# Fifteen places in the weight ring, and the last expert unit added into x by 0/1 products

## The chip, the core and the metric

The kernel runs on one core of one Trainium2 chip. The metric is device time in microseconds, median of three runs. TensorE (PE) multiplies, with its weight loads listed as PEld; VectorE (DVE), ScalarE (ACT) and GpSimd (POOL) do elementwise work; SyncE (SP) issues most DMAs. Each engine works through its own instructions in order.

## The reference

Two transformer blocks over 512 tokens of width 1024. The change lies in the mixture of experts that ends the first block: 32 experts, two for each token, each a SwiGLU of 1024 to 512 to 1024.

```python
def hierarchical_moe(h, ...):              # h: 512 tokens x 1024
    g_idx = argmax(h @ w_rg + b_rg)        # one of 4 groups
    top_val, top_loc = top_k(e_logits of that group, 2)   # 2 of its 8 experts
    gates = softmax(top_val) * g_gate
    # per expert e: every token that chose it
    out = (silu(x @ w_gate[e]) * (x @ w_up[e])) @ w_down[e] * gate
    return sum over a token's two experts

def first_block(x, ...):
    x = x + gate_a * mix                   # adaLN, mLSTM heads and pooling, w_out
    x = x + gate_f * hierarchical_moe(rms_norm(x, norm2_g) * (1 + scale_f) + shift_f, ...)
    return rms_norm(x, final_g)

def second_block(x, ...):                  # per layer: mixer (gMLP, then attention) and SwiGLU
    x = x + gmlp_mixer(rms_norm_2(x, a_norm[0]), ...)
    ...
    return rms_norm_2(x, final_norm)
```

## The kernel before

The activations lie transposed in `xT`, [128, 8, 512]. The stages follow one another: a mixer (adaLN modulation, mLSTM heads, pooling, output projection), the router, the experts, an overflow loop, the combination with x, then gMLP, SwiGLU, attention and SwiGLU. The order on each engine is the order in which the Python code records the instructions; waits are put in between by the framework.

`route` writes the normalised tokens to DRAM (`h2d`, L1283), ranks the experts by load and makes tables: `gidx`, which token sits in each row of a unit, `sidx`, the row of `y2` to which its output goes, `ordi`, the place of each expert's weights. The 32 experts make 19 units of 128 rows (`UNITS`, NU = 19): thirteen units hold two experts of up to 64 tokens, six a single one. The first unit holds two fixed experts, whose weights can be loaded before the router is done. Tokens beyond a unit's rows go to `overflow` (L1578), a loop with a run-time count, which is zero for these inputs.

The weights of an expert are six tiles of 1 MB: four for gate and up (`gu`), two for the projection down (`down`), 192 tiles in all. `Ring` (L309) loads them on SP's queue into 12 places (the names t, r and w are buffers that other stages use as well); a tile is loaded when the tile 12 ahead of it in the ring's order has been used on PE. `fill` reads the expert's place from `ordi` on SP before the expert's first load.

In `experts` (L1485) unit n is gathered from `h2d` by an indirect DMA on POOL (`gather`, three buffers `xg`), turned on PE (`x_t`), multiplied by gate and up (`gu`), gated on ACT and DVE, turned again (`act_t`), multiplied by `down`; DVE multiplies each half by the gate row of the modulation into `yo`, and an indirect DMA on POOL writes the rows of `yo` to `y2` in DRAM, [1024, 1024]: a row for each token and each of its two choices (`scatter`). The products down of unit n stand behind gate and up of unit n + 1; those of the last unit come at the end.

After the loop, `combine` (L1633) reads `y2` back as eight tiles of 128 rows `ya` on the queues of SP and ACT. For each of four token tiles, `tile(t)` adds the two choices (POOL, the last one DVE), turns the sum on PE (L1659), adds it into `xT` (DVE), and splits the new x into a high and a low part (`ht`: ACT, then DVE), which gMLP's products need. `ahead` (L1700) calls `tile` between the first gMLP products, so tile t + 1 is handled while the products of tile t run. `Stream` (`ws`, L214) loads and splits the other stages' weights; the first two tiles of gMLP are loaded behind the ring's last.

Of the kernel before, what the change touches and what calls it, by code (L numbers as in the profile page):

```python
# [308 lines left out]
class Ring:  # L309


    PLACES = ("t0", "t1", "r1", "w2", "w3", "r0", "w0", "w1", "r2", "r3", "t2", "t3")

    def __init__(self, K):
        self.K, self.order, self.loaded, self.used, self.at, self.tiles = K, [], 0, 0, {}, {}
        self.order = [(p, c) for c in range(6) for p in UNITS[0]]
        for n in range(1, NU + 1):
            for cs, u in ((range(4), n), ((4, 5), n - 1)):
                if 0 < u < NU:
                    self.order += [(p, c) for c in cs for p in UNITS[u]]  # L320

    def fill(self, most=1000):
        K = self.K
        while self.loaded < min(most, len(self.order), self.used + len(self.PLACES)):
            i = self.loaded
            p, c = self.order[i]
            t = self.tiles[i] = K.sb(self.PLACES[i % len(self.PLACES)], [128, 2048])
# [6 lines left out]
            K.nc.sync.dma_start(t, src)  # L334
# [21 lines left out]
class Kern:  # L356
# [331 lines left out]

    def load_late(self):
# [7 lines left out]
    def mixer(self):  # L697
# [72 lines left out]
        for j in range(DT):  # L770
# [10 lines left out]
            if j == 3:  # L781
                self.load_late()
            if j == 7:
# [478 lines left out]
    def route(self):  # L1262
# [21 lines left out]
        self.xg = [self.slot(i, [128, D]) for i in range(3)]  # L1284
# [19 lines left out]
        sel = self.slot(9, [128, NT, 4, 8])  # L1304
# [35 lines left out]
        rkt = self.slot(9, [128, 2, NT, 32])  # L1340
# [4 lines left out]
        rkt = self.slot(9, [128, 2, NT, 32])  # L1345
# [17 lines left out]
        pay = self.slot(10, [128, 8, 2, NU], F32R)  # L1363
# [24 lines left out]
        self.ts(self.gidx, tab[:, 224:224 + NU], 1024.0, None, OP.add)  # L1388
        self.ts(self.sidx, tab[:, 224 + NU:224 + 2 * NU], 1024.0, None, OP.add)
# [3 lines left out]
        def later():  # L1393
# [18 lines left out]
            table(oh0.bitcast(F32), tab[:, 264:264 + NU], lambda k, t: unit[:, 1, k * NT + t])  # L1412
            self.gates = self.sb("gates", [128, NU + 96])
# [71 lines left out]
    def experts(self):  # L1485

        nc = self.nc
        self.y2 = self.dr.tile([2 * S, D], F32, name="y2")
# [16 lines left out]
        def x_t(n):  # L1505
            b = self.ps(1)
            x = self.xg[n % 3]
            for k in range(8):
                nc.tensor.transpose(b[:, k // 4, (k % 4) * 128:(k % 4) * 128 + 128], x[:, k * 128:(k + 1) * 128], self.const("ident"))
            t = XT[n] = self.slot(3 + n % 2, [128, D])  # L1510
            self.turned(t, b)

        def products(n, out, lhs, first, last):
# [3 lines left out]
            for i in range(4):  # L1517
                for t, p in zip(ts, c):
                    self.mm(out[p], lhs[:, i * 128 + p.start:i * 128 + p.stop], t[:, i * 512:i * 512 + 512], first and i == 0, last and i == 3)
# [6 lines left out]
        def act_t(n):  # L1526
# [4 lines left out]
            t = ACT[n] = self.slot(5 + n % 2, [128, 512])  # L1531
            self.act(t, b)

        def down(n):
# [576 lines left out]
```

## Time and profile before

| | us |
|---|---|
| median of three runs | 1924.69 (1922.97 to 1930.77) |
| the profiled execution | 1929.17 |
| its span in the profile | 1927.4 |
| PE busy | 1813.0 (94%) |
| DVE busy | 848.8 (44%) |
| ACT busy | 593.0 (31%) |
| POOL busy | 146.0 (8%) |

The profile follows one execution. The busy share is an average over stages with different limits: the mixer (to about 260 us) is a mesh of short waits among all engines, the experts (about 283 to 771 us) are a stream of weights, and from about 800 us PE runs nearly without gaps to the end. What a change in one stage is worth is read from that stage's own rows.

### The profile page before, as it was taken

The page shows a single profiled execution, that of the slowest core. Times are in us where ns is not written, and L with a number is a line of the kernel's source. Part 1 is how long each engine was busy: PE and PEld are TensorE (multiplying, and loading weights), DVE is VectorE, ACT ScalarE, POOL GpSimd, SP SyncE. Part 2 cuts the span into 40 slices and gives each one's busy share as a digit, 9 for nine tenths or more (in the row PEclk, how much of TensorE's full clock was granted, in tenths as well). Part 3 has the DMA queues.
Part 4 walks back from the last instruction along what each step waited for, and adds up shares of the span by engine and source line. Part 5 has one row for each costly group of instructions (what it writes and reads, how often), then busy time and mean ns, then how long its engine had stood idle before and what let it go on. Part 6 is the DMA issues. An engine that isn't in the chain of part 4 may idle for free.

```text
span 1927.4 us, 20923 instructions
## 1 busy us (share of the span) xinstructions
PE 1813.0 (94%) x8054; PEld 1267.0 (66%) x8054; DVE 848.8 (44%) x1566; ACT 593.0 (31%) x1054; POOL 146.0 (8%) x119
## 2 busy tenths in 40 slices
PE   5988779999999898699999999999999999999997
PEld 4856654434333333588888888888778788888885
DVE  7657851111121111767644334436555654424434
ACT  4556430000000000444423223226666433212221
POOL 3443320000000000200000000000000000000000
PEclk9988879999999999899999999999999999999998
DMA  7533579999999998422232322222111132222321
GB/s 242 214 110 131 214 288 417 420 420 420 421 420 419 418 417 346 176 88 88 87 110 88 109 88 88 99 77 88 66 66 66 66 110 88 94 104 88 109 77 55
DMA packets 61240, 360.92 MB, mean 187 GB/s; under 512 B 9730, under 2 KB 9762, under 8 KB 23763
## 3 DMA queue, kind: packets, MB, share of 16 engines
q1 hardware_dynamic: 54000, 347.78, 46.6%
q0 software_dynamic: 5696, 8.64, 1.3%
q10 hardware_dynamic: 1442, 3.15, 0.4%
q8 instruction: 64, 1.05, 0.2%
q14 instruction: 38, 0.30, 0.1%
HBM read 356.91 MB, written 14.16 MB: 193 GB/s over the span
## 4 chain that ended last, share of the span: by engine, by line
PE 58%; DVE 1%; DMA 1%; ACT 0%; issue 0%; ACTq 0%; POOL 0%; DVEq 0%; POOLq 0%
PE q L394 57%; PE q L1988 0%; DMA a<-y 0%; PE q L465 0%; DVE a L414 0%; DVE t L406 0%; DMA y<-a,sidx 0%; DVE w L414 0%; DVE xT L406 0%; PE q L1659 0%; DVE ht L414 0%; POOL a L1656 0%; DVE a L406 0%; ACT t L403 0%; ACTq L1645 0%
## 5 line engine op out<-in xcount | busy, mean ns | idle before, releaser
L394 PE MATMUL q<-t,w 128*128 128x512 f32 (+1 forms) x3192 | 767.3, 397 | 7.4 <-DVE t L406 2.6
L394 PEld LDWEIGHTS q<-t,w 128*128 128x128 f32 (+1 forms) x3192 | 596.1, 189 | 150.6 <-issue 16.2
L406 DVE TENSOR_TENSOR w<-r,w 128x1024 fp32r<-128x1024 f32 (+1 forms) x173 | 208.6, 1226 | 312.2 <-ACT w L403 312.1
L394 PE MATMUL q<-a,w 128*128 128x512 f32 x1440 | 339.1, 395 | 0.0
L394 PEld LDWEIGHTS q<-a,w 128*128 128x128 f32 x1440 | 269.6, 188 | 63.6 <-issue 1.0
L403 ACT ACTIVATE w<-r 128x1024 fp32r<-128x1024 f32 (+1 forms) x173 | 177.1, 1049 | 347.3 <-issue 177.9
L394 PE MATMUL q<-r,a 128*64 128x512 f32 (+4 forms) x576 | 207.4, 580 | 10.3 <-DMA r<-in_we 8.9
L394 PE MATMUL q<-w,a 128*64 128x512 f32 (+1 forms) x512 | 186.1, 596 | 11.3 <-DMA w<-in_we 10.6
L403 ACT ACTIVATE a<-q 128x512 f32<-128x512 f32 (+2 forms) x82 | 37.2, 482 | 453.1 <-PE q L1530 358.4
L394 PE MATMUL q<-t,a 128*64 128x512 f32 (+1 forms) x512 | 145.9, 600 | 8.9 <-DMA t<-in_we 7.9
L414 DVE SCALAR_TENSOR_TENSOR a<-a,gates,q 128x512 f32<-128x512 f32 x19 | 14.2, 747 | 282.8 <-PE q L394 282.8
L394 PEld LDWEIGHTS q<-r,a 128*64 128x64 f32 (+1 forms) x576 | 69.6, 150 | 97.9 <-issue 77.0
L394 PEld LDWEIGHTS q<-w,a 128*64 128x64 f32 (+1 forms) x512 | 61.4, 147 | 93.3 <-issue 71.5
L394 PE MATMUL q<-w,t 128*128 128x256 f32 (+1 forms) x672 | 122.0, 336 | 0.0
L394 PEld LDWEIGHTS q<-w,t 128*128 128x128 f32 x672 | 102.8, 191 | 17.9 <-issue 4.1
L394 PEld LDWEIGHTS q<-t,a 128*64 128x64 f32 (+1 forms) x512 | 50.1, 147 | 92.1 <-issue 72.3
L406 DVE TENSOR_TENSOR a<-q,sqt 128x512 f32<-128x512 f32 x38 | 26.3, 692 | 116.1 <-PE q L394 116.1
L403 ACT ACTIVATE a<-ht 128x512 fp32r<-128x512 f32 (+1 forms) x60 | 37.8, 633 | 99.3 <-DVE ht L406 74.6
L406 DVE TENSOR_TENSOR xT<-q,xT 128x512 f32<-128x512 f32 x64 | 43.8, 687 | 52.9 <-PE q L394 43.5
L414 DVE SCALAR_TENSOR_TENSOR w<-r,cols,w 128x256 fp32r<-128x256 f32 x96 | 44.4, 480 | 39.3 <-ACT w L403 39.1
L403 ACT ACTIVATE ht<-ht 128x512 f32<-128x512 f32 x48 | 30.1, 631 | 87.3 <-DVE ht L406 87.3
L1471 POOL DMA_INDIRECT y<-a,sidx x19 | 20.9, 1098 | 450.6 <-DVE a L406 340.7
(325 smaller groups left out, 1398.0 us busy)
## 6 DMA issues: line engine op xcount, KB each, us to landing
r<-in_w SPq DMA_DIRECT2D x100, 1024.0 KB, 4.9
t<-in_we SPq DMA_DIRECT2D x64, 1024.0 KB, 20.9
r<-in_we SPq DMA_DIRECT2D x64, 1024.0 KB, 20.9
w<-in_we SPq DMA_DIRECT2D x64, 1024.0 KB, 20.4
r<-in_w_ada SPq DMA_DIRECT2D x48, 512.0 KB, 5.0
r<-in_wa SPq DMA_DIRECT2D x8, 466.0 KB, 8.9
r<-in_w SPq DMA_DIRECT2D x5, 512.0 KB, 3.5
xT<-in_x SPq DMA_DIRECT2D x4, 512.0 KB, 4.4
```

What stands on the lines that cost most here:

```text
L394: self.nc.tensor.matmul(out, lhsT=l, rhs=r, start=start, stop=stop)
L403: return self.nc.scalar.activation(out, in_, f, **kw)
L406: return self.nc.vector.tensor_tensor(out=out, in0=a, in1=b, op=op)
L414: return self.nc.vector.scalar_tensor_tensor(out, a, s, b, op0=op0, op1=op1, **kw)
L1471: self.nc.gpsimd.indirect_dma_start(out=self.y2[:, :], out_offset=bass.IndirectOffsetOnAxis(ap=idx, axis=0), in_=y, in_offset=None, bounds ...
```

## The change

The ring gets three more places, each made of two slots of 512 KB, loaded by two DMAs. To free the slots, other buffers become fewer or move: two gather buffers for three, one buffer for the turned input, `yo` in slots 5 and 3, the router's scratch in other names. The ring's order changes at the end: the products down of unit 17 come ahead of gate and up of unit 18.

The outputs of the last unit are not scattered. A 0/1 matrix `hot` (row of the unit by token, from the new table `tok`) turns and places them by a product on PE that is added to the turned sum of the other units' rows in the same bank. `y2` is read back, on SP, before the last `down`, and the sums of the two choices move from POOL to DVE. As the last unit's rows of `y2` are now not written, `y2` is cleared in the mixer (`clear`). The overflow loop adds its outputs to `xT` in the same manner and stands behind the addition into x; `combine` keeps the split alone. Two loads of gMLP move from SP's queue to POOL's.

```diff
 class Ring:
-    PLACES = ("t0", "t1", "r1", "w2", "w3", "r0", "w0", "w1", "r2", "r3", "t2", "t3")
+    PLACES = ("t0", "t1", "r1", "w2", "w3", "r0", "w0", "w1", "r2", "r3", "t2", "t3", ("a8", "a9"), ("a10", "a11"), ("a6", "a7"))
...
-        for n in range(1, NU + 1):
-            for cs, u in ((range(4), n), ((4, 5), n - 1)):
-                if 0 < u < NU:
-                    self.order += [(p, c) for c in cs for p in UNITS[u]]
+        parts = [(range(4), 1)]
+        for n in range(2, NU - 1):
+            parts += [(range(4), n), ((4, 5), n - 1)]
+        for cs, u in parts + [((4, 5), NU - 2), (range(6), NU - 1)]:
+            self.order += [(p, c) for c in cs for p in UNITS[u]]
...
+            if isinstance(tags, str):
+                t = K.sb(tags, [128, 2048])
+                K.nc.sync.dma_start(t, src)
...
+            else:
+                self.tiles[i] = []
+                for h, tag in enumerate(tags):
+                    t = K.sb(tag, [128, 1024])
+                    K.nc.sync.dma_start(t, src[:, h * 1024:(h + 1) * 1024])
+                    self.tiles[i] += [t[:, :512], t[:, 512:]]
...
+    def clear(self):
+
+        self.y2 = self.dr.tile([2 * S, D], F32, name="y2")
+        for i in range(8):
+            self.nc.scalar.dma_start(self.y2[i * 128:(i + 1) * 128], self.zero)
...
             if j == 3:
                 self.load_late()
+                self.zero = self.slot(9, [128, D])
+                nc.gpsimd.memset(self.zero, 0.0)
...
                 self.act(vT[t][:, :, 129 * i:129 * i + 128], v[:, :, i])
+        self.clear()
...
+            self.ts(self.tok, tab[:, 224:224 + NU], 1024.0, None, OP.add)
...
-        self.nc.gpsimd.indirect_dma_start(out=self.xg[n % 3], out_offset=None, in_=self.h2d[:, :],
+        self.nc.gpsimd.indirect_dma_start(out=self.xg[n % 2], out_offset=None, in_=self.h2d[:, :],
...
-            t = XT[n] = self.slot(3 + n % 2, [128, D])
+            t = XT[n] = self.slot(2, [128, D])
...
-            self.scatter(yo, self.sidx[:, i:i + 1])
+                if g == 0 and between:
+                    between()
+            if n < NU - 1:
+                self.scatter(yo, self.sidx[:, i:i + 1])
+            return yo
...
-        self.ws.stop = self.wide + 2
-        self.ws.fill()
-        act_t(NU - 1)
-        down(NU - 1)
-        self.ws.hold = len(self.ws.order)
-        self.ws.run()
+
+        n = NU - 1
+        act_t(n - 1)
+        down(n - 1)
+        i = UCOL[UNITS[n][0]]
+        hot = self.sb("W", [128, S], bufs=2)
+        self.onehot(hot, self.tok[:, i:i + 1])
+        banks = self.ps(0)
+        gu(n, 0, banks)
+        gu(n, 1, banks)
+        gate(n, banks)
+        ya = [[self.slot((8, 9, 10, 11, 6, 7, 0, 1)[2 * t + k], [128, D]) for k in range(2)] for t in range(NT)]
+        for t in range(NT):
+            if t % 2 == 0:
+                self.ws.stop = self.wide + 1 + t // 2
+                self.ws.fill()
+            for k in range(2):
+                nc.sync.dma_start(ya[t][k], self.y2[k * S + t * 128:k * S + (t + 1) * 128])
+        act_t(n)
+
+        def split():
+            self.ws.hold = len(self.ws.order)
+            self.ws.run()
+
+        yo = down(n, split)
+        for t in range(NT):
+            c = slice(t * 128, (t + 1) * 128)
+            b = Pair(*[self.bank(i) for i in ((0, 1), (6, 7))[t % 2]])
+            for a in range(2):
+                y, y2 = (ya[t][k][:, a * 512:a * 512 + 512] for k in range(2))
+                self.tt(y, y, y2, OP.add)
+                for i in range(4):
+                    k = slice(a * 512 + i * 128, a * 512 + i * 128 + 128)
+                    self.mm(b[:, a, i * 128:i * 128 + 128], ya[t][0][:, k], self.const("ident"), True, False)
+                    self.mm(b[:, a, i * 128:i * 128 + 128], yo[:, k], hot[:, c], False, True)
+                x = self.xT[:, 4 * a:4 * a + 4, c]
+                self.tt(x, b[:, a].rearrange("p (b t) -> p b t", b=4), x, OP.add)
+
+    def onehot(self, out, tok):
+
+        for t in range(NT):
+            self.ts(out[:, t * 128:(t + 1) * 128], self.const("slots"), tok, -128.0 * t, OP.subtract, OP.is_equal)
...
     def combine(self):
...
-                (nc.vector if (t, a) == (3, 1) else nc.gpsimd).tensor_tensor(out=y, in0=y, in1=y2, op=OP.add)
-            for a in range(2):
-                for i in range(4):
-                    nc.tensor.transpose(b[:, a, i * 128:i * 128 + 128], ya[t][0][:, a * 512 + i * 128:a * 512 + i * 128 + 128],
-                                        self.const("ident"))
-                self.tt(xs[a], b[:, a].rearrange("p (b t) -> p b t", b=4), xs[a], OP.add)
+            xs = [self.xT[:, 2 * i:2 * i + 2, c] for i in range(4)]
...
-        nc.sync.dma_start(wsp.rearrange("p g t -> p (g t)"), self.ap["wsp"])
-        nc.sync.dma_start(bsp, self.bc(self.ap["rows"], 36, D))
+        nc.gpsimd.dma_start(wsp.rearrange("p g t -> p (g t)"), self.ap["wsp"])
+        nc.gpsimd.dma_start(bsp, self.bc(self.ap["rows"], 36, D))
```

Where instructions now stand. ACT, in the mixer behind the evictions of v (a4, a5 hold v, w2 is a part of the next weights, bp a bias column). Before:

```order
L403 ACTIVATE a5_91_527<-q0_98_536 128x2x128 x2
L403 ACTIVATE a5_91_527<-q1_99_537 128x2x128 x2
L403 ACTIVATE w2_114_726<-r1_102_544 128x1024 x2
L403 ACTIVATE a10_88_521<-q2_117_734 128x512
L403 ACTIVATE a2_94_532<-q3_118_735,bp_119_772,cols_2_68 128x512
L403 ACTIVATE a6_122_780<-q6_120_776 128x512
```

Now:

```order
L416 ACTIVATE a5_92_529<-q0_99_538 128x2x128 x2
L416 ACTIVATE a5_92_529<-q1_100_539 128x2x128 x2
L706 DMA y2_728<-a9_73_352 128x1024 x8
L416 ACTIVATE w2_115_737<-r1_103_546 128x1024 x2
L416 ACTIVATE a10_89_523<-q2_118_745 128x512
L416 ACTIVATE a2_95_534<-q3_119_746,bp_120_783,cols_2_68 128x512
L416 ACTIVATE a6_123_791<-q6_121_787 128x512
```

Eight DMAs from the zeroed slot a9 to y2 stand between the last eviction of v and the split of the weights.

SP, at the router's end (a4 to a7 are the normalised tokens, t0 and t1 the first places of the ring). Before:

```order
L1283 DMA h2d_1792<-a6_302_1831 128x1024
L1283 DMA h2d_1792<-a7_305_1845 128x1024
L332 TENSOR_LOAD ordi_338_1952
...
L334 DMA t0_353_2014<-in_we 128x2048
...
L334 DMA t1_354_2025<-in_we 128x2048
```

Now:

```order
L1305 DMA h2d_1803<-a6_303_1842 128x1024
L1305 DMA h2d_1803<-a7_306_1856 128x1024
L336 TENSOR_LOAD ordi_339_1962
...
L346 DMA a8_344_1993<-in_we 128x1024
...
L346 DMA a9_345_1995<-in_we 128x1024
...
L346 DMA a10_346_1997<-in_we 128x1024
...
L346 DMA a11_347_1999<-in_we 128x1024
...
L346 DMA a6_348_2001<-in_we 128x1024
...
L346 DMA a7_349_2003<-in_we 128x1024
...
L340 DMA t0_360_2044<-in_we 128x2048
```

Between the reading of `ordi` and the next load into t0 now stand six loads into a8, a9, a10, a11, a6 and a7.

DVE, at the end of the experts (sqt is the gate row, fa a gain, w2 and w3 the split weights of gMLP). Before, ahead of the overflow loop:

```order
L406 TENSOR_TENSOR a10_748_4095<-q6_746_4093,sqt_341_1971 128x512
L406 TENSOR_TENSOR a10_748_4095<-q7_747_4094,sqt_342_1972 128x512
L406 TENSOR_TENSOR a9_755_4130<-q6_753_4128,sqt_341_1971 128x512
L406 TENSOR_TENSOR a9_755_4130<-q7_754_4129,sqt_342_1972 128x512
L414 SCALAR_TENSOR_TENSOR w3_757_4153<-r1_749_4117,fa_14_95,w2_756_4152 128x512 x4
L1581 TENSOR_LOAD overi_664_3673
```

and behind it (t0 to t3 are the low parts for gMLP):

```order
L406 TENSOR_TENSOR xT_4_72<-q6_806_4330,xT_4_72 128x4x128
L406 TENSOR_TENSOR xT_4_72<-q7_807_4331,xT_4_72 128x4x128
L406 TENSOR_TENSOR t0_788_4309<-xT_4_72,t0_788_4309 128x2x128
L406 TENSOR_TENSOR t1_789_4310<-xT_4_72,t1_789_4310 128x2x128
L406 TENSOR_TENSOR t2_790_4311<-xT_4_72,t2_790_4311 128x2x128
L406 TENSOR_TENSOR t3_791_4312<-xT_4_72,t3_791_4312 128x2x128
L406 TENSOR_TENSOR xT_4_72<-q0_808_4352,xT_4_72 128x4x128
L406 TENSOR_TENSOR xT_4_72<-q1_809_4353,xT_4_72 128x4x128
```

Now, ahead of the loop:

```order
L419 TENSOR_TENSOR a5_801_4233<-q6_799_4231,sqt_342_1980 128x512
L427 SCALAR_TENSOR_TENSOR w3_803_4244<-r1_795_4212,fa_14_95,w2_802_4243 128x512 x4
L419 TENSOR_TENSOR a5_801_4233<-q7_800_4232,sqt_343_1981 128x512
L419 TENSOR_TENSOR a8_787_4204<-a8_787_4204,a9_788_4205 128x512
L419 TENSOR_TENSOR xT_4_72<-q0_804_4262,xT_4_72 128x4x128
L419 TENSOR_TENSOR a8_787_4204<-a8_787_4204,a9_788_4205 128x512
L419 TENSOR_TENSOR xT_4_72<-q1_805_4263,xT_4_72 128x4x128
L419 TENSOR_TENSOR a10_789_4206<-a10_789_4206,a11_790_4207 128x512
L419 TENSOR_TENSOR xT_4_72<-q6_806_4284,xT_4_72 128x4x128
```

The weight split has moved ahead of the second gate product; sums of rows (a8 with a9, a10 with a11) alternate with additions into xT, four token tiles of two halves each, and all of them stand ahead of the loop, with the low parts behind it.

On PE each half tile is now four products of the summed rows with the identity and four of the last unit's outputs (a5) with `hot`, in turn, into one bank.

## Rows read from the trace of the kernel before

**Rows 1.** The page: 40 slices of the span; granted clock in tenths, then GB/s.
```profile
PEclk9988879999999999899999999999999999999998
...
GB/s 242 214 110 131 214 288 417 420 420 420 421 420 419 418 417 346 176 88 88 87 110 88 109 88 88 99 77 88 66 66 66 66 110 88 94 104 88 109 77 55
```

**Rows 2.** Waits of SP's queue: who waited for whom, total us, times, longest.
```profile
SPq L332 <- DVE ordi L1391: 7.9, 1, 7.9
```

**Rows 3.** Timeline around the router's end: start, us, engine, line, operation, [idle before <-releaser].
```profile
275.71 0.17 DVE L1391 CAST ordi<-q 1x32 int32<-1x32 f32 x1
...
276.92 1.15 POOL L1466 DMA_INDIRECT a<-h2d,gidx  x1 [8.32 <-DMA h2d<-a]
...
281.36 1.94 PE L1509 MATMUL q<-cst,a 128*128 128x128 f32 x8 [3.46 <-DMA a<-h2d,gidx]
...
287.74 0.96 SPq L334 DMA_DIRECT2D t<-in_we  x2
```

**Rows 4.** Windows there: us, busy of PE, PEld, DVE, ACT, POOL; PEclk, DMA share, GB/s.
```profile
275.00:280.00 5.00, 2.46 (x11) 1.95 (x10) 0.34 (x3) 2.46 (x3) 2.47 (x3) 0.50 0.20 53
280.00:285.00 5.00, 3.64 (x14) 2.13 (x16) 1.81 (x6) 0.42 (x2) 0.68 (x1) 0.51 0.57 167
285.00:290.00 5.00, 5.00 (x26) 1.65 (x24) 1.29 (x6) 0.00 (x0) 0.00 (x0) 1.00 0.20 56
```

**Rows 5.** Tile h2d over the run (19 gathers, four writes): times to landing.
```profile
DMA to landing us min/median/max: 4.3/10.1/13.1
```

**Rows 6.** Timeline in the mixer, behind the products for v.
```profile
106.32 2.06 ACT L403 ACTIVATE w<-r 128x1024 fp32r<-128x1024 f32 x2
...
113.41 6.23 PE L394 MATMUL q<-a,small 128*128 128x512 f32 x10 [2.78 <-ACT gcols L403]
...
119.67 0.60 ACT L403 ACTIVATE a<-q 128x512 f32<-128x512 f32 x1 [0.26 <-PE q L394]
```

**Rows 7.** Tile y: ACT's issues of the reads of y2, ns min/median/max.
```profile
L1645 ACTq DMA_DIRECT2D a<-y x6: 326/406/511, 775.8 to 781.3; - x6
```

**Rows 8.** Timeline from the last pair of expert tiles to the gapless gmlp.
```profile
767.43 3.65 PE L394 MATMUL q<-t,a 128*64 128x512 f32 x14 [1.00 <-SPq L1582]
...
770.08 2.56 ACT L403 ACTIVATE w<-r,fa 128x512 fp32r<-128x512 f32 x4 [8.20 <-DMA r<-in_w]
...
771.12 0.69 DVE L406 TENSOR_TENSOR a<-q,sqt 128x512 f32<-128x512 f32 x1 [4.74 <-PE q L394]
...
775.77 5.82 ACTq L1645 DMA_DIRECT2D a<-y  x6
...
787.41 4.26 PE L394 MATMUL q<-w,t 128*128 128x512 f32 x12
...
797.63 0.68 DVE L1656 TENSOR_TENSOR a<-a,a 128x512 f32<-128x512 f32 x1
...
798.46 0.63 PE L1659 MATMUL q<-cst,a 128*128 128x128 f32 x4 [2.69 <-DVE a L1656]
...
798.84 15.22 PE L394 MATMUL q<-w,t 128*128 128x512 f32 x66
...
798.95 0.73 ACT L403 ACTIVATE t<-xT 128x256 fp32r<-128x256 f32 x2 [2.07 <-DVE xT L406]
...
799.13 0.69 DVE L406 TENSOR_TENSOR xT<-q,xT 128x512 f32<-128x512 f32 x1 [0.21 <-PE q L1659]
...
799.73 1.42 DVE L406 TENSOR_TENSOR t<-xT,t 128x256 fp32r<-128x256 f32 x4
```

**Rows 9.** Chain that ended last: the last scatter (start, us, what).
```profile
772.09 2.77 DMA y<-a,sidx
```

**Rows 10.** Timeline in the mixer: eight 4-byte products of 128x128 at full clock.
```profile
176.54 1.05 PE L394 MATMUL q<-a,a 128*128 128x129 f32 x8
```

**Rows 11.** Windows of the old tail, columns as in rows 4.
```profile
776.00:781.00 5.00, 0.00 (x0) 0.00 (x0) 0.00 (x0) 0.00 (x0) 0.99 (x1) 0.55 0.81 269
781.00:785.00 4.00, 2.69 (x10) 1.89 (x11) 1.91 (x4) 1.22 (x4) 2.80 (x3) 0.50 1.04 404
```

More of the change, by code (lines that the diff above doesn't have):

```diff
@@ L326, in fill @@
             p, c = self.order[i]
-            t = self.tiles[i] = K.sb(self.PLACES[i % len(self.PLACES)], [128, 2048])
+            tags = self.PLACES[i % len(self.PLACES)]
             if p >= 30:
@@ L333, in fill @@
                 src = K.ap["we"][bass.ds(self.at[p] + c, 1)].rearrange("o p c -> (o p) c")
-            K.nc.sync.dma_start(t, src)
+            if isinstance(tags, str):
+                t = K.sb(tags, [128, 2048])
+                K.nc.sync.dma_start(t, src)
+                self.tiles[i] = [t[:, k * 512:(k + 1) * 512] for k in range(4)]
+            else:
[4 more added lines that the diff above has]
+                    self.tiles[i] += [t[:, :512], t[:, 512:]]
             self.loaded += 1
@@ L1283, in route @@
             nc.sync.dma_start(self.h2d[t * 128:(t + 1) * 128], ht)
-        self.xg = [self.slot(i, [128, D]) for i in range(3)]
+        self.xg = [self.slot(i, [128, D]) for i in range(2)]
         for x in self.xg:
@@ L1303, in route @@
         og, gm = first_max(L[:, :, 0:4], 4, self.const("first4"), "rg")
-        sel = self.slot(9, [128, NT, 4, 8])
+        sel = self.sb("unit", [128, NT, 4, 8])
         ogb = og.unsqueeze(3).to_broadcast([128, NT, 4, 8])
@@ L1518, in products @@
                 for t, p in zip(ts, c):
-                    self.mm(out[p], lhs[:, i * 128 + p.start:i * 128 + p.stop], t[:, i * 512:i * 512 + 512], first and i == 0, last and i == 3)
+                    self.mm(out[p], lhs[:, i * 128 + p.start:i * 128 + p.stop], t[i], first and i == 0, last and i == 3)
             self.ring.done(len(c))
@@ L1530, in act_t, with down @@
                 nc.tensor.transpose(b[:, k * 128:k * 128 + 128], a[:, k * 128:(k + 1) * 128], self.const("ident"))
-            t = ACT[n] = self.slot(5 + n % 2, [128, 512])
+            t = ACT[n] = self.sb("gs", [128, 512])
             self.act(t, b)
-        def down(n):
+        def down(n, between=None):
             t = ACT.pop(n)
             b = self.ps(2)
-            yo = self.slot(9 + n % 2, [128, D])
+            yo = self.slot((5, 3)[n % 2], [128, D])
             i = UCOL[UNITS[n][0]]
@@ L1541, in down, with gate @@
                 self.tt(yo[:, g * 512:(g + 1) * 512], b[:, g], self.gf[g], OP.mult)
-            self.scatter(yo, self.sidx[:, i:i + 1])
+                if g == 0 and between:
[3 more added lines that the diff above has]
+            return yo
+        def gate(n, banks):
+            sg = self.slot(4, [128, 2, 512])
+            i = UCOL[UNITS[n][0]]
+            self.act(sg[:, 0], banks[:, 0], AF.Silu)
+            self.stt(sg[:, 1], sg[:, 0], self.gates[:, i:i + 1], banks[:, 1], OP.mult, OP.mult)
+            ACT[n] = sg[:, 1]
         x_t(0)
@@ L1546, in experts @@
         next(late)
-        for n in range(NU):
+        for n in range(NU - 1):
             banks = self.ps(0)
@@ L1627, in overflow @@
                 for k in range(4):
-                    self.mm(yb[:, g], at[:, k * 128:k * 128 + 128], w[:, k * 512:(k + 1) * 512], k == 0, k == 3)
-            yo = self.slot(9, [128, D])
+                    self.mm(yb[:, g], at[:, k * 128:k * 128 + 128], w[k], k == 0, k == 3)
+            yo, hot = self.slot(10, [128, D]), self.slot(11, [128, S])
             self.gated(yo, yb, ga)
-            self.scatter(yo, si[:, 0:1])
-    def combine(self):
-        nc = self.nc
-        ya = [[self.slot(2 * t + k, [128, D]) for k in range(2)] for t in range(NT)]
-        for t in range(NT):
-            n = 2 if t < 2 else 1
-            for a in range(n):
-                c = slice(a * D // n, (a + 1) * D // n)
-                for k in range(2):
-                    (nc.sync if k else nc.scalar).dma_start(ya[t][k][:, c], self.y2[k * S + t * 128:k * S + (t + 1) * 128, c])
+            self.onehot(hot, tok)
+            for d in range(DT):
+                b = self.bank(4 + d % 2)
+                self.mm(b, yo[:, d * 128:(d + 1) * 128], hot, True, True)
+                self.tt(self.xT[:, d], b, self.xT[:, d], OP.add)
+    def combine(self):
         self.ws.stop = len(self.ws.order)
```

50 lines of the change are left out of this document (23 added, 27 removed).

## The prediction

> **What bounds the kernel now.** I read the 40-slice table first. From slice 6 to slice 14 (290 to 720 us) the DMA engines move 417 to 421 GB/s without a break [rows 1]: the expert stage is paced by its 192 weight tiles of 1 MB, at 1.049 MB / 420 GB/s = 2.5 us a tile. Ahead of that there is a hole: while the router finishes and the first rows are gathered, the three windows from 275 to 290 us move 53, 167 and 56 GB/s [rows 4]. Of those 15 us, 15 - 5 x 276 / 420 = 11.7 us are unused. SP sits there because all 12 places are full and the next load waits for PE: the table of expert numbers is ready at 275.9 us (SP waits 7.9 us for it [rows 2]), but the next weight load goes out at 287.74 [rows 3].
>
> At the far end I follow the timeline. The last pair of tiles starts on PE at 767.43 (call it T) and takes 3.65; then come the product with the gate row, the scatter, the empty overflow loop, the reads of y2, and four tiles of add, transposition and add to x [rows 8]. The scatter lands at 774.86 [rows 9] and ACT's first read is issued at 775.77. From 798.84 PE runs without gaps. Two groups of 12 products were done before that (the first is in the rows), and a product then costs 15.22 / 66 = 0.231 us, so the old tail is worth a gapless start at T + 31.4 - 24 x 0.231 = **T + 25.9**. PE is the bound after it, so a shift here goes through to the end.
>
> **The change part by part.**
>
> *Three more places.* Tiles 12 to 14 no longer wait for PE. SP issues them as six halves right after the table is read, from about 276 us, into the hole, which can hold them: 3 x 2.5 = **7.5 us** is the most that the DMA-paced stage can start ahead. Against it stands the gather of the first unit's rows. It leaves POOL at 276.92 and PE starts on it at 281.36 [rows 3], on idle DMA engines. Now three tiles run beside it. Landings of gathers and their neighbours run from 4.3 us (idle) to a median of 10.1 (weights streaming) [rows 5], so the first release of a place comes 0 to 5.8 us later, and the hole after the three tiles is longer by that. The tiles start less than a microsecond ahead of the gather and come in halves, so I stay below the middle and take 2.7. Ring: 2.7 - 7.5 = **-4.8**, between -7.5 and -1.7. The Trainium skill ("DMA: Bandwidth & Descriptors", section "Queues, rings and completion order") says that a DMA engine takes turns between its queues, one packet at a time. With the gather waiting for one or two turns of half a tile (1.25 us each, my estimate by that page) it would cost 1.3 to 2.5 us and the forecast would be 0.2 to 1.4 us lower; the rows' 5.8 us says that a gather loses more than that under a full stream.
>
> The other edits of the loop cost nothing that I can find: two gather buffers for three (gather 2 now waits for the first transposition, and its rows are wanted two units later), one buffer for the turned input (its writer already stood behind the products that read the old one, on PE), new slots for outputs. The cover is the DMA stream; without it each would be a fraction of a microsecond per unit.
>
> *Clearing y2.* Rows of the last unit are no longer scattered, so y2 is zeroed first: a memset on POOL, and eight DMAs of 512 KB issued **by ACT**, between the evictions of v and the split of the next weights. An issue on ACT takes 0.406 us in the median, up to 0.511 [rows 7]: with the spacing 8 x 0.44 = 3.5 us in which ACT does nothing else. Behind them stand ACT's split of the weights (106.32), DVE's subtraction for it, DVE's small product bp, ACT's evictions that wait for bp, and PE, which waits 2.78 us for ACT's gcols at 113.41 [rows 6]. So it lies on the path, and nothing behind it has a clock of its own to hide it: **+3.5**. Bounds: 0 if a later wait takes it up, +6 if the 4.2 MB (10 us at 420 GB/s) land after 122.5, when ACT rewrites their source (119.67 before, plus the delay).
>
> *The tail.* The order on DVE decides it. Ahead of the second gate product now stand four pieces of a weight split. Their tile lands where it did (ACT starts on it at T + 2.65, 2.56 us for four), so DVE's last piece ends at T + 6.0 and the gate product at T + 6.7. Before, the gate product came first, at 771.12 [rows 8]. The reads of y2 queue behind that weight tile, two of 512 KB to a tile time: the first pair is in by T + 5.2, the last by T + 16. They are hidden. Then come eight steps, each strictly in a row: DVE adds two rows' halves (0.68), 0.15 until PE starts, eight 128x128 products, 0.04, DVE adds into x (0.69, of which 0.09 overlap the next) [rows 8]. The next sum stands behind the add into x on DVE, and all eight products behind the sum, so nothing overlaps: 1.47 us beside PE. Eight such products take 1.05 us at full clock [rows 10] and 1.94 at the lower one [rows 3]. PE idles from T + 3.65 to T + 7.5. After the same kind of pause in the old tail the granted clock fell to 0.55 and 0.50 and stayed at 0.50 through transpositions that filled two thirds of the window [rows 11]. In the new steps PE would be busy 1.94 of 3.41 us, less than that, so I take the lower clock (1.2 GHz): 8 x 3.41 = 27.3, end at T + 6.7 + 27.3 - 0.6 (first step partly fast) = T + 33.4. At the high level it is 8 x 2.52 = 20.2, T + 26.9.
>
> The overflow loop, empty here, stands now behind the last add and not behind the scatter: 775.77 - 774.86 = 0.9 us. Then ACT's first split (0.73 / 2) and DVE's (1.42 / 4), with hand-overs 0.9 [rows 8]: products start at T + 35.2 (28.7 at the high level). Starting at the lower clock costs some more: the first twelve took 4.26 us at 787.41 and not 12 x 0.231 = 2.8; with a rise no sooner, 2.2 us. New tail: **T + 37.4** against T + 25.9, **+11.5** (high level: +2.8). What is saved is the scatter and the wait for the reads, 771.8 to 780; what is paid is that four tiles no longer overlap each other, nor the first products.
>
> *Sum*: -4.8 + 3.5 + 11.5 = **+10.2 us**. On the profiled execution (1929.17 us, span 1927.4) that is 1939.4. That execution lies 4.5 us above the median of the three runs, and the difference carries over: 1924.69 + 10.2 = **1934.9 us**.
>
> **The rivals.**
>
> *The clock holds* (not slower): it does not fall in the pause and the steps keep it up; this decides if the granted clock stays 1.00 from T to the first gmlp product. Then -4.8 + 3.5 + 2.8 = +1.5, 1926.2; with the ring's gain at its bound of -7.5 it is -1.2, just under before. For it: in the weight stage, which waits for each tile, the granted clock is nine tenths or more throughout [rows 1]. Against it: [rows 11], where it fell during a pause and stayed low.
>
> *The clear is absorbed*: some later wait takes the 3.5 us. +6.7, 1931.4. Against it is PE's own wait for ACT there [rows 6].
>
> *The places gain nothing*: the gather pays as much as the worst row says, or the six halves go out late because slots a6 and a7 are still being read by the copies to h2d. Then the ring gives -1.7 to 0, and the sum is +13.3 to +15, 1938 to 1940.
>
> **How the numbers follow.** Something near 0.5%, 9.6 us, is what a measurement here can tell from no change, that is 1934.3, and my sum lies on that edge. The forecast has 0.62, of which 0.38 above the edge and 0.24 below; the clock holds 0.15 (no change); the clear is absorbed 0.10 (0.08 no change); the places gain nothing 0.08 (slower); 0.05 is left for a gain of over 0.5%, which even all favourable bounds together (-7.5 + 0 + 2.8 = -4.7, 1920) do not reach. Slower 0.48, same 0.47, faster 0.05. Bounds at one end: clock 1926.2 and up; at the other 1940 and the clear's +6. Leaving out a tenth on each side gives 1927 to 1941.
>
> **What the new profile would show.** *Ring*: six issues of we on SP between 276 and 279 us, no long idle window from 278 to 286, and the last pair of tiles on PE 1 to 6 us earlier against the start of the stage. If the gather's first transposition starts later than 4 us after its old distance from ordi, my 2.7 is too low. *Clear*: eight issues on ACT around 106 us, and gcols, the qk evictions and ordi all later by the same 3 to 4 us; if ordi is not later, the term falls. *Tail*: on DVE eight pairs of sum and add into x, 3.4 us from pair to pair with granted clock 0.5, or 2.5 with 1.0; the loop's branch after the eighth; the first gapless gmlp product 35 us after the last pair's start. *Wrong* would be a DVE that waits for reads of y2, or a gmlp that starts before the eighth add.

## The result, and the profile after

The changed kernel takes 1942.12 us (median of six runs, 1939.78 to 1946.61) and the kernel before 1927.81 (1922.97 to 1933.45): a ratio of 1.0081, interval 1.0066 to 1.0096. By the ratio that is 15.6 us slower; the two medians alone differ by 14.3. Slower by over 0.5% was the case to which I gave 0.48; the size was forecast too small, +10.2 us, and 1942.12 lies above the range. The changed kernel's profiled execution took 1940.75 us (span 1939.0), the one before 1929.17; between these two the difference is 11.6 us.

Three stretches of the profile after. First the mixer, timeline (start, us, engine, line, operation): the eight issues of the clear on ACT and what stands behind them, to set against [rows 6].

```profile
103.57 0.36 ACTq L706 DMA_DIRECT2D y<-a  x1
...
103.97 0.43 ACTq L706 DMA_DIRECT2D y<-a  x1
...
104.45 0.72 ACTq L706 DMA_DIRECT2D y<-a  x1
...
105.20 1.16 ACTq L706 DMA_DIRECT2D y<-a  x1
...
106.39 5.04 ACTq L706 DMA_DIRECT2D y<-a  x4
...
111.48 2.00 ACT L416 ACTIVATE w<-r 128x1024 fp32r<-128x1024 f32 x2 [5.34 <-issue]
...
118.23 0.23 ACT L416 ACTIVATE gcols<-q 128x48 f32<-128x48 f32 x1
```

ACT's split of the weights starts at 111.48 and not at 106.32, and PE's products behind gcols at 118.50 and not at 113.41. The first issues take 0.4 us, the last four 1.26 each. In the window from 105 to 110 us the DMA engines move 414 GB/s, about what they move in the weight stage [rows 1], and 0.52 MB at that rate is 1.27 us. So ACT issued at the pace at which the bytes moved. That an issue waits until an earlier transfer has moved is not shown by this, and the run with the clear on SP, below, speaks against it.

```profile
105.00:110.00 5.00, 5.00 (x20) 2.23 (x18) 0.00 (x0) 1.14 (x5) 0.00 (x0) 1.00 1.02 414
```

Then the router's end, against [rows 3].

```profile
281.12 0.17 DVE L1414 CAST ordi<-q 1x32 int32<-1x32 f32 x1
...
281.97 1.14 POOL L1490 DMA_INDIRECT a<-h2d,gidx  x1 [8.24 <-DVE ordi L1414]
...
282.30 3.46 SPq L346 DMA_DIRECT2D a<-in_we  x6
...
288.36 1.94 PE L1532 MATMUL q<-cst,a 128*128 128x128 f32 x8 [5.05 <-DMA a<-h2d,gidx]
...
294.57 1.48 SPq L340 DMA_DIRECT2D t<-in_we  x2
```

The six halves go out 1.2 us behind ordi, as forecast. The gather needs 6.39 us until PE starts on it, where it needed 4.44.

Last the tail, against [rows 8]: the last tile's products, the split, the gate product, the first sums and additions, and gmlp.

```profile
767.03 4.12 PE L407 MATMUL q<-t,gs 128*64 128x512 f32 x16
...
770.73 2.74 DVE L427 SCALAR_TENSOR_TENSOR w<-r,fa,w 128x512 fp32r<-128x512 f32 x4 [2.79 <-ACT w L416]
773.39 0.68 DVE L419 TENSOR_TENSOR a<-q,sqt 128x512 f32<-128x512 f32 x1
773.99 0.68 DVE L419 TENSOR_TENSOR a<-a,a 128x512 f32<-128x512 f32 x1
...
776.83 0.69 DVE L419 TENSOR_TENSOR xT<-q,xT 128x512 f32<-128x512 f32 x1 [2.16 <-PE q L407]
777.44 0.68 DVE L419 TENSOR_TENSOR a<-a,a 128x512 f32<-128x512 f32 x1
...
780.26 0.69 DVE L419 TENSOR_TENSOR xT<-q,xT 128x512 f32<-128x512 f32 x1 [2.14 <-PE q L407]
...
801.11 0.69 DVE L419 TENSOR_TENSOR xT<-q,xT 128x512 f32<-128x512 f32 x1 [2.21 <-PE q L407]
...
803.45 22.33 PE L407 MATMUL q<-w,t 128*128 128x512 f32 x90 [2.38 <-ACT t L416]
```

The steps are there: sum, products, addition, one after the other, 3.45 us from step to step. The windows (us, busy of PE, PEld, DVE, ACT, POOL; granted clock, DMA share, GB/s) say at which clock.

```profile
777.00:781.00 4.00, 2.05 (x16) 1.86 (x16) 1.86 (x4) 0.00 (x0) 0.00 (x0) 1.00 0.12 48
781.00:785.00 4.00, 2.02 (x16) 1.86 (x16) 1.84 (x3) 0.00 (x0) 0.00 (x0) 1.00 0.02 6
...
803.40:806.00 2.60, 2.55 (x6) 1.90 (x7) 2.28 (x7) 2.60 (x8) 1.03 (x2) 0.54 0.88 277
```

At 1.00 throughout, and not at the 0.50 that I had assumed. The clock fell only behind the last step: in the pause ahead of gmlp, from 801.8 to 803.4, it is still 1.00, and gmlp's first products run at 0.54. And a step has 16 matmul records for its eight products.

To compare profiles I use three distances. **Mixer**: when ordi is ready. **Ring**: from the start of the first gather to the end of the last tile's products (call that end E). **Tail**: from E to the start that gapless gmlp would have had, products done earlier counted at 0.231 us.

| | mixer | ring | tail |
|---|---|---|---|
| before, first profile | 275.7 | 494.2 | 22.2 |
| before, second profile | 271.9 | 493.5 | 22.4 |
| changed, first profile | 281.1 | 489.2 | 33.8 |
| changed, second profile | 282.2 | 490.4 | 35.3 |

For the tail of the changed kernel: 803.45 + 22.33 - 90 x 0.231 - 771.15 = 33.8; in my terms of T that is T + 37.5, where I had forecast T + 37.4.

### The profile page after: what moved, and what is told of

Its sections match the earlier page's. It is cut to its first block, busy times and chain, and to the rows that moved or that the text cites. A ratio compares the mean times of both kernels' runs of the same rounds, so it can differ in the third digit from the quotient of the medians.

```text
span 1939.0 us, 21277 instructions
## 1 busy us (share of the span) xinstructions
PE 1814.4 (94%) x8150; PEld 1273.1 (66%) x8150; DVE 853.5 (44%) x1578; ACT 592.9 (31%) x1054; POOL 136.4 (7%) x113
## 4 chain that ended last, share of the span: by engine, by line
PE 58%; DVE 1%; ACT 0%; issue 0%; DVEq 0%; ACTq 0%
PE q L407 57%; PE q L2041 0%; PE q L478 0%; DVE a L427 0%; DVE ht L427 0%; DVE xT L419 0%; DVE a L419 0%; DVE sqacc L419 0%; DVEq L2134 0%; ACT a L416 0%; ACT sqt L416 0%; DVE rst L427 0%; DVE rsy L427 0%; DVE rst L419 0%; ACT t L416 0%
## 5 line engine op out<-in xcount | busy, mean ns | idle before, releaser
L407 PE MATMUL q<-r,a 128*64 128x512 f32 (+4 forms) x360 | 156.0, 569 | 5.5 <-DMA r<-in_we 5.5
L427 DVE SCALAR_TENSOR_TENSOR a<-a,gates,q 128x512 f32<-128x512 f32 x19 | 14.2, 747 | 272.6 <-PE q L407 272.6
L407 PE MATMUL q<-w,a 128*64 128x512 f32 x296 | 105.8, 597 | 12.5 <-DMA w<-in_we 12.5
L416 ACT ACTIVATE gs<-q 128x512 f32<-128x512 f32 (+2 forms) x26 | 14.2, 546 | 337.6 <-PE q L1553 335.0
L407 PE MATMUL q<-t,a 128*64 128x512 f32 (+1 forms) x288 | 109.0, 601 | 5.9 <-DMA t<-in_we 5.2
L407 PE MATMUL q<-a,a 128*64 128x512 f32 (+7 forms) x400 | 91.4, 459 | 0.4 <-DVE mdn L1193 0.4
L407 PEld LDWEIGHTS q<-r,a 128*64 128x64 f32 (+1 forms) x360 | 53.6, 158 | 55.4 <-issue 42.8
L407 PEld LDWEIGHTS q<-t,a 128*64 128x64 f32 (+1 forms) x288 | 36.3, 154 | 63.9 <-issue 54.3
L407 PEld LDWEIGHTS q<-w,a 128*64 128x64 f32 x296 | 31.4, 137 | 59.8 <-issue 36.6
L416 ACT ACTIVATE a<-ht 128x512 fp32r<-128x512 f32 (+1 forms) x60 | 37.8, 632 | 99.3 <-DVE ht L419 74.6
L407 PEld LDWEIGHTS q<-a,a 128*128 128x128 f32 (+2 forms) x400 | 44.3, 176 | 29.1 <-issue 22.3
```

The costliest lines, as they stand in the source:

```text
L407: self.nc.tensor.matmul(out, lhsT=l, rhs=r, start=start, stop=stop)
L416: return self.nc.scalar.activation(out, in_, f, **kw)
L427: return self.nc.vector.scalar_tensor_tensor(out, a, s, b, op0=op0, op1=op1, **kw)
```

## The experiments

Ratios are to the kernel before, which ran on the same chip in between. Differences in us between two changed kernels are those of their ratios.

**The same two kernels again.**

> The changed kernel once more, beside the kernel before on one chip. Reading A (all of the difference lies in the three stages that the two profiles show: the clear +5.4, the ring -5.3, the tail +11.6): 11.6 / 1927.8 gives a ratio of 1.0060, and a second profile has the table ordi at 281 us, the last tile's products ending 490 us behind it, and gmlp's gapless products from 803 to 804. Reading B (something that the pair of profiles does not show adds some 3 us): a ratio near 1.0075 to 1.0081, and stages that differ from the first profile by as much.

Measured 1.0078 (1.0062 to 1.0094). Reading B holds: the runs say 15 us, the first pair of profiles 11.6. The second profile shows one of the missing parts. Its timeline has the first step 4.94 us long, from sum to sum, the second 3.44:

```profile
776.29 0.68 DVE L419 TENSOR_TENSOR a<-a,a 128x512 f32<-128x512 f32 x1
...
781.23 0.68 DVE L419 TENSOR_TENSOR a<-a,a 128x512 f32<-128x512 f32 x1
...
784.67 0.68 DVE L419 TENSOR_TENSOR a<-a,a 128x512 f32<-128x512 f32 x1
```

The granted clock in that first step is 0.57, and 1.00 in the second. So the lower clock does fall into the steps, in some executions. The profile of the kernel with twelve places, below, has it in two.

> The kernel before once more, for a second profile of its mixer and its tail. If the stages that the first profile showed are typical, ordi is at 275 to 277 us, the last tile's products end 494 us behind the first gather, and gapless gmlp is worth a start 22 us behind them; a profile that differs by several us says how much of a difference between two profiles is chance.

One run, 1924.68 us. This is the other missing part: ordi was 3.8 us earlier than in the first profile of the same code, with the same ring and tail. The mixer differs from execution to execution by several us, and my base, already 4.5 us above its median, had a late one.

**The clear on another engine.**

```diff
-            self.nc.scalar.dma_start(self.y2[i * 128:(i + 1) * 128], self.zero)
+            self.nc.sync.dma_start(self.y2[i * 128:(i + 1) * 128], self.zero)
```

> The changed kernel with the eight clearing DMAs issued by SP in place of ACT, at the same place of the program. Theory: the clear's whole price is ACT, which stood from 103.57 to 111.43 behind its own issues. Then ACT splits its weights at 106 again, ordi is ready at 275.5 to 276.5 in place of 281.1, and the time falls by 5 to 5.5 us against the changed kernel (0.9972). Rival 1: it is the 4.2 MB of writes that delay the stage, whoever issues them, because SP's next weight tile queues behind them: ordi stays at 280 to 281, no change. Rival 2: in between, SP's next load waits for its own issues and costs 2 to 3 us.

Measured 1.0047 (1.0031 to 1.0063), 6 us below the changed kernel. The timeline: SP now stands behind its own issues, and ACT does not.

```profile
99.37 6.29 SPq L706 DMA_DIRECT2D y<-a  x8
...
106.16 2.06 ACT L416 ACTIVATE w<-r 128x1024 fp32r<-128x1024 f32 x2
...
112.97 0.23 ACT L416 ACTIVATE gcols<-q 128x48 f32<-128x48 f32 x1
```

The theory holds; neither rival shows, since SP's next weight tile was not due before 109.69. But SP needed 0.79 us an issue, and had all eight out at 105.66, when the DMA engines had moved only some 1.6 MB since 99 us (234 GB/s over 6.7 us), the weight tile ahead included. So an issue need not wait for the transfer before it, and why ACT's burst kept to the DMA rate stays open. Over all profiles taken, ordi is ready at 277.3 to 282.2 us, mean 280.6, in the seven with the clear on ACT, at 273.9 to 278.0 in the four with it on SP, and at 271.9 to 275.8 in the three without it.

**Twelve places.**

```diff
-    PLACES = (..., "t2", "t3", ("a8", "a9"), ("a10", "a11"), ("a6", "a7"))
+    PLACES = (..., "t2", "t3")
```

> The changed kernel with the twelve old places only. Theory: the three places are worth the 5.3 us by which the stretch from ordi to the end of the last tile's products is shorter (490.0 after, 495.4 before): the stretch goes back to 495 and the time rises by 5 to 5.5 us (1.0027). Rival (the shorter stretch comes from the other order of the last two units or from the moved loads, not from the places): the stretch stays at 490 to 492 and the time within 2 us.

Measured 1.0101 (1.0084 to 1.0119), 4.4 us above the changed kernel. From the gather to E is 282.86 to 777.37, 494.5 us, as before the change.

```profile
282.86 1.15 POOL L1490 DMA_INDIRECT a<-h2d,gidx  x1 [8.40 <-DVE ordi L1414]
...
286.95 1.94 PE L1532 MATMUL q<-cst,a 128*128 128x128 f32 x8 [2.76 <-DMA a<-h2d,gidx]
...
773.21 4.16 PE L407 MATMUL q<-t,gs 128*64 128x512 f32 x16
```

So the places are what shortens the stretch, and the other order of the last units is not. The gather is at its old 4.1 us again. This kernel's profile also shows what a step costs at the lower clock (1.2 GHz): windows of the pause, two steps and a third.

```profile
777.00:780.30 3.30, 0.36 (x1) 0.00 (x0) 3.30 (x6) 1.78 (x3) 0.00 (x0) 0.99 0.94 302
780.30:785.40 5.10, 3.75 (x16) 3.49 (x16) 1.21 (x3) 0.00 (x0) 0.00 (x0) 0.50 0.45 186
785.40:790.50 5.10, 3.79 (x16) 3.49 (x16) 1.22 (x3) 0.00 (x0) 0.00 (x0) 0.50 0.05 19
790.50:794.00 3.50, 2.02 (x16) 1.86 (x16) 1.34 (x3) 0.00 (x0) 0.00 (x0) 1.00 0.00 0
```

Eight products take 3.8 us at 0.50 and 2.0 at 1.00; the step 5.17 and 3.45.

**The sums on POOL.**

```diff
-                self.tt(y, y, y2, OP.add)
+                self.nc.gpsimd.tensor_tensor(out=y, in0=y, in1=y2, op=OP.add)
```

> The changed kernel with the eight sums of two y rows on POOL in place of DVE. Theory (each of the eight steps is a strict row of sum, sixteen passes on PE, addition): POOL, which has nothing else to do, sums ahead, and the steps go at the pace of PE: from 3.45 us a step to 2.0 to 2.2, eight steps 17 us in place of 27, the time 9 to 11.5 us lower (0.9945). Rival 1 (the steps wait for the reads of y2, or POOL at 1.3 to 1.5 us a sum comes too late for the first ones): 4 to 7 us. Rival 2 (PE's time in the steps is set by a low clock): the passes take longer than 2.0 us for eight products and less than 5 us is gained.

Measured 1.0017 (1.0006 to 1.0028), 11.8 us below the changed kernel: the serial row on DVE was the tail's cost. The additions into x now follow each other at 1.79 us, PE's own pace for eight products, and the tail is 21.6 us.

```profile
771.62 3.78 DVE L427 SCALAR_TENSOR_TENSOR w<-r,fa,w 128x512 fp32r<-128x512 f32 x4 [2.81 <-ACT w L416]
...
773.60 5.38 POOL L1630 TENSOR_TENSOR a<-a,a 128x512 f32<-128x512 f32 x4 [29.28 <-DMA a<-y]
...
778.57 0.69 DVE L419 TENSOR_TENSOR xT<-q,xT 128x512 f32<-128x512 f32 x1 [2.57 <-PE q L407]
...
780.36 0.69 DVE L419 TENSOR_TENSOR xT<-q,xT 128x512 f32<-128x512 f32 x1 [1.09 <-PE q L407]
```

**The gate product ahead of the split.**

```diff
-        yo = down(n, split)
+        yo = down(n)
+        split()
```

> The changed kernel with the four pieces of the weight split behind the second gate product on DVE, not ahead of it. Theory (DVE's row is the chain, so whatever stands ahead of the gate product counts): the first sum ends 2.7 us earlier behind the last tile's products, but the split then stands ahead of the first sum on the same engine, so the chain to the first sum is as long as before: no change, within 1 us, ratio 1.0075 to 1.0081, with the gate product right behind PE (0.05 us after the last tile) and the first sum still 2.9 us behind it. Rival (PE's products of the last unit's outputs, which need the gate product alone, are what ends last): 2.7 us less, ratio 1.0064.

Measured 1.0089 (1.0075 to 1.0103): no gain.

```profile
770.74 0.69 DVE L419 TENSOR_TENSOR a<-q,sqt 128x512 f32<-128x512 f32 x1 [3.27 <-PE q L407]
...
774.00 0.69 DVE L419 TENSOR_TENSOR a<-a,a 128x512 f32<-128x512 f32 x1
```

The gate product moves to 770.74, 0.04 behind E, and the first sum still starts 3.3 us behind E, at 774.00. It is the length of DVE's row that counts, not the place of one piece in it. My prediction's sentence that the split ahead of the gate product costs was right in its sum and would have been wrong as advice.

**A longer pause.** Twelve memsets of 128x1024 ahead of the first sum.

> The changed kernel with twelve memsets of 128x1024 on DVE (some 7 us in all) between the gate product and the first sum, so that PE stands still for some 11 us in place of 3.6. Theory (the granted clock falls while PE stands still, for a time, and what falls into that time runs at half speed): the clock shows 0.50 in the pause and through one to three of the steps, which take 5.16 us each, and 1.00 after; the time rises by 7 us for the memsets and 1.7 for each slow step. Rival (the steps themselves, in which PE is busy for 1.9 of 3.45 us, cannot bring the clock back): all eight steps take 5.16, and the time rises by 7 + 13.7.

One run, 1957.93 us. The memsets took 14.0 us (0.91 each and 0.28 between two), twice my guess. What the run was for is in its windows: the pause, the first step and the second.

```profile
780.00:785.00 5.00, 0.00 (x0) 0.00 (x0) 3.88 (x5) 0.00 (x0) 0.00 (x0) 0.50 0.04 16
...
789.60:793.50 3.90, 3.75 (x16) 3.49 (x16) 0.01 (x1) 0.00 (x0) 0.00 (x0) 0.50 0.00 0
793.50:797.00 3.50, 2.05 (x16) 1.86 (x16) 1.36 (x3) 0.00 (x0) 0.00 (x0) 0.98 0.00 0
```

PE stood still for 17.7 us, the clock fell to 0.50, and one step of sixteen records without a gap later it was back. The rival, that the steps cannot bring it back, falls, and with it my argument from [rows 11]: there the work between two gaps was 1.1 us, and the clock stayed low.

**The tail in another order, and with the clear on SP.** The loop moves ahead of the reads of y2, the sums to POOL, the gate product ahead of the split, and the additions into x between the first gmlp products, as the kernel before has them. The loop's buffers and two loads of gMLP move with it (not printed).

```diff
         gate(n, banks)
+        self.overflow()
...
+                nc.gpsimd.tensor_tensor(out=y, in0=y, in1=y2, op=OP.add)
...
-        yo = down(n, split)
+        self.hot, self.yo = hot, down(n)
+        split()
...
         def tile(t):
+            for a in range(2):
+                for i in range(4):
+                    self.mm(b[:, a, i * 128:i * 128 + 128], self.ya[t][0][:, k], self.const("ident"), True, False)
+                    self.mm(b[:, a, i * 128:i * 128 + 128], self.yo[:, k], self.hot[:, c], False, True)
+                self.tt(x, b[:, a].rearrange("p (b t) -> p b t", b=4), x, OP.add)
```

> The changed kernel with its tail in another order: the overflow loop ahead of the reads of y2, the sums on POOL, the gate product ahead of the split, and the eight half tiles, each with its split of x, between the first gmlp products as before the change. Theory: nothing is then in a row but PE's own products, 8 x 1.8 us, so gapless gmlp is worth a start 0.7 + 14.4 + 2 to 4 us of gaps behind the last tile's end, 17 to 19 us, where the changed kernel has 33.9 (805.0 - 771.1) and the kernel before 22.2: 15 to 17 us less than the changed kernel, ratio 0.9995 to 1.0005. Rival 1 (the loop, now ahead of the reads, holds SP until DVE reaches it, and the stream of weights gets a hole): the last tile ends 2 to 5 us later, ratio 1.001 to 1.003. Rival 2 (the lower clock falls on the products and each half tile takes 3.8): 5 us worse.

Measured 1.0013 (1.0004 to 1.0022). The tail is shorter than I expected, 14.2 us, and rival 1 takes it back: E lies 498.5 us behind the gather and not 490.

> The kernel of the pipelined tail with the clear on SP as well. If the two prices add up (5.5 to 6 for the clear on ACT, 15 to 17 for the order of the tail), the ratio is 0.997, that is 5 to 7 us faster than the kernel before: the ring's gain of 4.5 to 5.3 is then left, with 3 to 5 us of a shorter tail, less what the loop costs. If the tail only takes back what it lost, it is 1.000 or above.

Measured 0.9980 (0.9968 to 0.9991), faster than the kernel before. The hole, in this kernel's waits of SP (who waited for whom, total us, times, longest), its windows and its timeline:

```profile
SPq L1641 <- SPq L1641: 18.7, 8, 2.6
```

```profile
757.00:760.00 3.00, 0.63 (x2) 0.00 (x0) 0.75 (x1) 0.00 (x0) 0.00 (x0) 1.00 0.26 104
760.00:763.00 3.00, 0.00 (x0) 0.00 (x0) 0.00 (x0) 0.00 (x0) 0.00 (x0) 1.00 0.07 30
763.00:766.00 3.00, 1.11 (x4) 0.71 (x4) 0.00 (x0) 0.49 (x1) 0.00 (x0) 0.50 0.01 5
```

```profile
764.36 1.11 PE L1553 MATMUL q<-cst,a 128*128 128x128 f32 x4 [6.73 <-SPq L1641]
```

At the loop SP waits eight times between 745 and 764 us, never longer than 2.6 us, which is the time of a tile; I read that as the loads under way, one after the other. PE waits 6.73 us for SP, though the gated input that it is to turn was ready at 758.5. Hardly anything is loaded in between. The next kernel, which leaves the loop behind the additions, has no such hole: there E lies 489.6 us behind the gather.

**Three edits, the loop left where it is.** The clear on SP, the sums on POOL, the gate product first.

> The changed kernel with three edits: the clear on SP, the sums on POOL, the gate product ahead of the split; the loop stays behind the additions into x. If the prices that the single runs showed add up (clear 6.0, sums 11.8 us below the changed kernel at 15) and the gate product, with the sums no longer on DVE, now gives its 2.7 to 3.3 us, the time is 20 to 21 us below the changed kernel and 5 to 6 below the kernel before: ratio 0.9965 to 0.9975. Gapless gmlp is then worth a start 18 to 20 us behind the last tile's end. If the gate product gives nothing here either (the split, slowed by POOL's additions, holds DVE's additions into x), 0.9985.

Measured 0.9990 (0.9979 to 1.0001), near the second case, in which the gate product gives nothing. The tail is 23.4 us, 1.2 longer than before the change.

```profile
768.49 0.69 DVE L419 TENSOR_TENSOR a<-q,sqt 128x512 f32<-128x512 f32 x1 [3.19 <-PE q L407]
769.10 4.75 DVE L427 SCALAR_TENSOR_TENSOR w<-r,fa,w 128x512 fp32r<-128x512 f32 x4
770.00 6.21 POOL L1631 TENSOR_TENSOR a<-a,a 128x512 f32<-128x512 f32 x4 [29.14 <-DMA a<-y]
...
771.68 0.79 PE L407 MATMUL q<-cst,a 128*128 128x128 f32 x2 [3.22 <-POOL a L1631]
```

Now the reads of y2, which I had called hidden, end last: POOL waits for the first pair until E + 1.5, and needs 1.55 us a sum beside the split. gmlp's first product starts 21.4 us behind E, as in the run that has only the sums on POOL, so the gate product's place gains nothing. Here it starts at the lower clock (0.82 from 790 to 793; there 1.00 from 793.4 to 796), and the tail is 1.8 us longer than there.

**The ring alone.** The three places and the buffers that make room for them, put into the kernel before; no clear, the old tail.

> The kernel before with the three places alone: the ring's half tiles and the buffers that make room for them; no clear, the last unit scattered, the old order of the last units, the old tail. Theory: the stretch from the first gather to the end of the last tile's products falls from 494 to about 490 us, and nothing else changes: 4 to 4.5 us less than the kernel before, ratio 0.9977 to 0.9979. Rival (the old tail takes it back, because its pause, its scatter and its reads hang on a time of their own): within 1.5 us of the kernel before, ratio 0.9992 to 1.0008.

Measured 0.9979 (0.9965 to 0.9992), 4 us faster; the gather starts at 276.64, E is 766.61, 490.0 us later, the tail 22.3. The theory holds.

```profile
276.64 1.15 POOL L1475 DMA_INDIRECT a<-h2d,gidx  x1 [8.72 <-DVE ordi L1400]
...
762.96 3.65 PE L403 MATMUL q<-t,gs 128*64 128x512 f32 x14 [0.93 <-SPq L1591]
```

> The kernel of the pipelined tail and the clear on SP once more, beside the kernel with the ring alone on one chip. It measured 0.998; its parts as the traces show them are the ring's 4 to 4.5 us, a tail that is worth a gapless start 14 us behind the last tile in place of 22, and a hole of 7 to 8 us ahead of the last tile where the loop waits for every load under way. If that account is right it comes out within 2 us of the ring alone, ratio 0.997 to 0.999.

Measured 0.9975 (0.9964 to 0.9987), 1922.7 us beside 1923.54 for the ring alone. Both beat both given kernels; between them there is no difference to be seen. Gather to E is 497.4 us, the tail 14.2: the hole ahead of the last tile eats the gain of the tail, as the account said. Whether the loop can stand where it makes no hole and holds up no tail was not tried.

## Why the prediction was right or wrong

| term | forecast | shown |
|---|---|---|
| ring | -4.8 | -4 to -5 |
| clear | +3.5 | +5.1 at gcols, 6.0 in time |
| tail | +11.5 | +11.6 in the first profile, +13 to 15.5 in four others |
| sum | +10.2 | +15.0 to 15.6 |

Two terms of the sum were too small: the clear, where the price of an issue failed, and the tail, where the price of a step was misread and an execution with slow steps costs more than I allowed. The base moved against me as well.

**The ring: right in mechanism and size.** The stretch shrinks from 494 us to between 489 and 490, the kernel with twelve places gives 4.4 us back, the ring alone gains 4. The gather's loss, which I took at 2.7, is 6.39 - 4.44 = 1.95. A gain of 4 to 5 and a loss of 2 make the three tiles worth 6 to 7 us, less than the 7.5 that I called the most: both parts were a little high, and they cancel. By the rule of the Trainium skill that I quoted ("DMA: Bandwidth & Descriptors", section "Queues, rings and completion order") I had estimated 1.3 to 2.5; this trace agrees with it, and with 2.35 in the ring alone. The other profiles with the three places have 1.8 to 2.5, but for the one with the sums on POOL: 3.7.

**The clear: the mechanism right, the size wrong.** The step that failed is 8 x 0.44 us. I took the price of an issue from [rows 7], where six reads were spread over 5.5 us. That is 1.1 us from one start to the next, and I took only the 0.4 that a single one lasts. On ACT the eight writes of 0.52 MB held it for 7.9 us, 1.16 to 1.26 each after the first three; on SP they took 6.3. The number to set beside it was the DMA rate: 4.2 MB at 420 GB/s is 10 us. I had that number and used it only for the landing. What makes an issue wait is not shown. The rival that a later wait absorbs it falls.

**The tail: the sum right for the wrong reason, and the reason matters.** I read [rows 10] as eight products in 1.05 us. They are records, and a product of two 4-byte operands has two: in the changed kernel 16 records stand for eight products. At full clock they take 1.8 to 2.0 us, not 1.05, and at half 3.8, not 1.94. I then chose the lower clock, which made 1.94 out of 1.05 and came within 0.1 us of what the full clock gives. So the rival "the clock holds" came true in its condition (1.00 in all eight steps of the first profile) and was wrong in its price, 2.52 us a step for 3.45. What my forecast could not hold is the third state: a step at the lower clock takes 5.17, and other executions have one or two of them, +1.7 us each. Three more profiles of this tail (twelve places, the clear on SP, the gate product first) have 36.2 to 37.8 us. So the step that failed in the forecast of the tail is the price of eight products; what the runs showed in its place is 3.45 us a step at full clock and up to two steps of 5.17. The Trainium skill ("FP8 and Floating Point Precision", section "TensorE Precision Notes") says that a product in true FP32 passes the array four times. The trace agrees: 0.22 us for a product of 128 columns, where one of 512 columns in gmlp takes 0.231, so 0.058 for 128 columns in one pass, a factor of 3.8.

**That nothing overlaps within the row of sum, products and addition was the cause, and it is shown**: the sums on POOL alone give 11.8 us back. "They are hidden", of the reads of y2, was right in the changed kernel and stops being right as soon as the row on DVE is shorter. The loop's price, 0.9 us, was about right where the change put it; its real price shows when loads are under way.

**The base.** I carried the 4.5 us between the profiled execution and the median over as chance, which the second profile of the kernel before bears out: there 3.8 us lie in the mixer. The three runs that I had seen give 1924.69, the medians with more runs lie at 1926.6 to 1928.0; that moved the time by 2 to 3 us against my range, which was too narrow for it.

## What to carry to other kernels

Before counting an issue as 0.4 us, set the bytes of the burst against the DMA rate, and give the burst to an engine that has time to stand. Where a step goes DVE, PE, DVE and the next begins on the same DVE, look for an engine with nothing to do that can work ahead: here one changed word gave back 11.8 us. And when the price of a product is read from records, count first how many records a product has: here two for each product of 4-byte operands.

## What the runs showed of the hardware that I had not expected

- A loop with a run-time count, run zero times, held SP for 18.7 us in eight waits and PE for 6.73 us, with the DMA engines down to 5 GB/s behind it, in a stretch where DMA was the bound. The last tile came 7 to 9 us later for it.
- An addition on POOL slows DVE beside it: the four pieces of the split take 2.74 us alone, 3.78 and 4.75 beside POOL's sums, and POOL's sums 1.55 in place of 1.26. The Trainium skill ("SBUF — State Buffer", section "SBUF: two separate sides") says that the two share a port that one holds for a whole instruction while the other blocks; the trace agrees that both lose time, and no run here shows the port itself.
- The same tail had its granted clock at 0.50 in none, one or two of eight steps, behind a pause on PE of 3.6 us (4.1 with the gate product first). After 17.7 us of standing still it needed one step to come back.
